# Rotary embedding in fp32: GpSimd and VectorE share the arithmetic in place of bf16 arithmetic between ScalarE casts

## The chip, the cores and the metric

One Trainium2 chip, one of its cores. The metric is the device time of one execution in microseconds (us), the median of several. All runs quoted here are of the fast state, at a granted clock of 1.0. The profile shows a span from the first to the last instruction. DVE is VectorE, ACT is ScalarE, POOL is GpSimd, SP is SyncE. SBUF and PSUM are the on-chip memories in which the kernels' tiles lie. The profile leaves numbers out of tile names: its t_ps and t_sb are the kernel's t1_ps and t2_sb.

## The reference

```python
x: (16, 512, 1024) fp32          # batch, seq, 16 heads of 64
cos, sin: (512, 32) fp32
x = x.reshape(16, 512, 16, 64)
x1, x2 = x[..., :32], x[..., 32:]
c, s = cos[None, :, None, :], sin[None, :, None, :]
out = concatenate([x1 * c - x2 * s, x1 * s + x2 * c], axis=-1)   # fp32
```

33.55 MB are read and 33.55 MB are written, whatever the arithmetic. Each element takes two multiplications and one addition or subtraction. A *row* below is one sequence position in each of the 128 partitions, an SBUF tile of 128x1024 fp32 (512 KB). There are 64 rows.

## The kernel before

A tile is one batch: four rows, 2 MB. The last two batches are split into two and four pieces. SyncE loads, ScalarE casts fp32 to bf16, VectorE does four bf16 operations, ScalarE casts back to fp32 and issues the store.

```python
# (cut: tile list, buffers, semaphores)
@block.sync
def _(sp):
    for t in range(NT):
        ...
        if t >= NX:                              # NX = 3 buffers of x
            sp.wait_ge(sem_ci, t - NX + 1)       # cast of the tile that held it
        sp.dma_start(x_sb[:, xb, 0:E], x_tile_ap(t)).then_inc(sem_in[xb], 16)
        ...                                      # t == 0: cos and sin after it
@block.scalar
def _(ae):
    ...                                          # tables to bf16
    for it in range(NT + LEAD):                  # LEAD = 2
        ...
            ae.wait_ge(sem_vf, u + 1)
            ...
            ae.activation(o_sb[:, ob, 0:Eu], ob_sb[:, obb, 0:Eu], ACT_COPY).then_inc(sem_co, 1)   # L129
            ae.wait_ge(sem_co, u + 1)
            ae.dma_start(out_tile_ap(u), o_sb[:, ob, 0:Eu]).then_inc(sem_out[ob], 16)
        ...
            ae.activation(xb_sb[:, cb, 0:E], x_sb[:, xb, 0:E], ACT_COPY).then_inc(sem_ci, 1)      # L143
@block.vector
def _(ve):
    for t in range(NT):
        ...
        ve.tensor_tensor(t1v, xbv, cos_b, mult)                              # bf16, L170
        ve.tensor_tensor(t2v, xbv, sin_b, mult).then_inc(sem_vp, 1)          # bf16, L171
        ...
        ve.tensor_tensor(obv[:, :, 0:HALF], t1[:, :, 0:HALF], t2[:, :, HALF:HD], subtract)
        ve.tensor_tensor(obv[:, :, HALF:HD], t2[:, :, 0:HALF], t1[:, :, HALF:HD], add).then_inc(sem_vf, 1)
```

## Time and profile before

| | before |
|---|---|
| measured time, median | 163.84 us |
| span of the profiled run | 162.1 us |
| busy: VectorE, ScalarE, GpSimd | 111.3, 118.6, 0.2 us |
| moved | 67.26 MB, 415 GB/s over the span |

First the profile page's busy times, then its slices. The span is cut into 40 equal slices of 4.05 us. Each digit is the busy share of a slice in tenths, 9 meaning 90% or more, and the last line is what the DMA engines moved in each.

```profile
DVE 111.3 (69%) x80; ACT 118.6 (73%) x45; POOL 0.2 (0%) x4
...
DVE  0006997989898989896939488492966994635450
ACT  3078389898989898967588775868859787445552
...
DMA  5999999999999999999999999999999999999985
GB/s 158 417 429 449 421 421 412 429 437 421 437 437 425 433 437 421 437 437 425 433 437 417 441 437 414 441 437 417 441 417 427 437 421 444 436 409 423 426 360 212
```

The DMA row is a solid line of nines from the second slice to the 38th, at 410 to 450 GB/s. No other row is. The engines that compute have gaps everywhere. This kernel is limited by its transfers.

The chain of waits agrees in its second half. It follows back what the last instruction depended on. First its shares of the span by engine, then a stretch of it; the columns are start, length and what it was.

```profile
DMA 54%; ACT 30%; issue 7%; DVE 5%; ACTq 1%; SPq 0%; DVEq 0%
...
66.12 24.16 DMA x_sb<-in_x_dram
90.28 0.02 issue
90.30 3.63 ACT xb_sb L143
93.93 0.02 issue
93.95 25.51 DMA x_sb<-in_x_dram
```

These two loads last 24 and 26 us, because three loads at a time and the stores share what the DMA engines moved, 431 GB/s from 60 to 100 us (loads land 9.7 us apart here, at 70.8, 80.6 and 90.3 us; the median of all 2 MB loads is 16.8 us). One cast (3.63 us) frees a buffer, and the next load starts at once. In the first half, up to 66 us, the chain runs through ScalarE instead, from cast to cast: it has 30% of the whole. Which of the two limits the kernel, the chain alone does not settle; the copy without arithmetic, e4 below, does.

Two groups of instructions on the page show what the change takes away (busy time in us, then the mean of one in ns):

```profile
L143 ACT ACTIVATE xb_sb<-x_sb 128x4096 bf16<-128x4096 f32 (+2 forms) x20 | 58.7, 2933 | 19.9 <-DMA x_sb<-in_x_dram 17.1
...
L129 ACT ACTIVATE o_sb<-ob_sb 128x4096 f32<-128x4096 bf16 (+2 forms) x20 | 58.6, 2929 | 12.7 <-DMA out_dram<-o_sb 7.5
```

The casts are 117 us of ScalarE work. What ended most of ScalarE's idle time is in both lines a DMA: ScalarE waits for transfers. But the load queue waits for casts too, in total (us), times, and longest wait:

```profile
SPq L100 <- ACT xb_sb L143: 132.3, 17, 10.3
```

Each load needs the buffer that a cast frees, so each side waits for the other. The DMA row shows that the DMA engines were kept busy all the same.

### The profile page before, as it was taken

How to read it: one execution, taken by the hardware profiler on the slowest of the kernel's cores; microseconds unless marked ns; L12 is line 12 of the kernel's file. 1: busy time of each engine (PE TensorE's matmuls, PEld its weight loads, DVE VectorE, ACT ScalarE, POOL GpSimd, SP SyncE). 2: the span in 40 equal slices, each digit the busy share in tenths (PEclk: the TensorE clock that was granted, in tenths of full speed). 3: DMA queues.
4: the chain of work that ended last, by engine and by line, in shares of the span. 5: the costliest groups of instructions: out<-in, count | busy, mean ns of one | idle time of the engine just before them, and what ended most of it. 6: DMA issues, size and time to landing. Idle time of an engine off the chain costs nothing.

```text
span 162.1 us, 266 instructions
## 1 busy us (share of the span) xinstructions
DVE 111.3 (69%) x80; ACT 118.6 (73%) x45; POOL 0.2 (0%) x4
## 2 busy tenths in 40 slices
DVE  0006997989898989896939488492966994635450
ACT  3078389898989898967588775868859787445552
POOL 0000000000000000000000000000000000000000
DMA  5999999999999999999999999999999999999985
GB/s 158 417 429 449 421 421 412 429 437 421 437 437 425 433 437 421 437 437 425 433 437 417 441 437 414 441 437 417 441 417 427 437 421 444 436 409 423 426 360 212
DMA packets 6050, 67.26 MB, mean 415 GB/s; under 512 B 672, under 2 KB 928, under 8 KB 1952
## 3 DMA queue, kind: packets, MB, share of 16 engines
q1 hardware_dynamic: 3168, 33.69, 49.5%
q10 hardware_dynamic: 2880, 33.56, 48.6%
q14 instruction: 2, 0.02, 0.0%
HBM read 33.69 MB, written 33.55 MB: 415 GB/s over the span
## 4 chain that ended last, share of the span: by engine, by line
DMA 54%; ACT 30%; issue 7%; DVE 5%; ACTq 1%; SPq 0%; DVEq 0%
DMA x_sb<-in_x_dram 49%; ACT xb_sb L143 15%; ACT o_sb L129 14%; DMA sin_sb<-in_sin_dram 5%; DVE tmp_sb L171 2%; DVE tmp_sb L170 1%; ACTq L133 1%; DVE ob_sb L176 1%; DVE ob_sb L179 1%; SPq L102 0%; SPq L100 0%; DVEq L55 0%; ACT coscat_sb L112 0%; ACT sincat_sb L115 0%; ACT coscat_sb L113 0%
## 5 line engine op out<-in xcount | busy, mean ns | idle before, releaser
L143 ACT ACTIVATE xb_sb<-x_sb 128x4096 bf16<-128x4096 f32 (+2 forms) x20 | 58.7, 2933 | 19.9 <-DMA x_sb<-in_x_dram 17.1
L170 DVE TENSOR_TENSOR tmp_sb<-xb_sb,coscat_sb 128x4096 bf16<-128x4096 bf16 (+2 forms) x20 | 37.3, 1865 | 45.8 <-ACT xb_sb L143 45.8
L129 ACT ACTIVATE o_sb<-ob_sb 128x4096 f32<-128x4096 bf16 (+2 forms) x20 | 58.6, 2929 | 12.7 <-DMA out_dram<-o_sb 7.5
L171 DVE TENSOR_TENSOR tmp_sb<-xb_sb,sincat_sb 128x4096 bf16<-128x4096 bf16 (+2 forms) x20 | 37.1, 1857 | 0.0
L176 DVE TENSOR_TENSOR ob_sb<-tmp_sb 128x2048 bf16<-128x2048 bf16 (+2 forms) x20 | 20.2, 1011 | 0.7
L179 DVE TENSOR_TENSOR ob_sb<-tmp_sb 128x2048 bf16<-128x2048 bf16 (+2 forms) x20 | 20.1, 1004 | 0.0
L112 ACT ACTIVATE coscat_sb<-cos_sb 128x128 bf16<-128x128 f32 x1 | 0.3, 309 | 7.0 <-DMA sin_sb<-in_sin_dram 7.0
L112 ACT ACT_TABLE_LOAD x1 | 1.3, 1283 | 0.7 <-PEq L197 0.7
L113 ACT ACTIVATE coscat_sb<-cos_sb 128x128 bf16<-128x128 f32 x1 | 0.3, 293 | 0.0
L115 ACT ACTIVATE sincat_sb<-sin_sb 128x128 bf16<-128x128 f32 x1 | 0.3, 293 | 0.0
L114 ACT ACTIVATE sincat_sb<-sin_sb 128x128 bf16<-128x128 f32 x1 | 0.3, 292 | 0.0
L197 POOL MEMSET const-bfloat16-1.0<- 128x1 bf16 x1 | 0.1, 101 | 0.0
L197 POOL MEMSET const-uint8-127<- 128x1 uint8 x1 | 0.1, 101 | 0.0
L197 POOL MEMSET const-float32-0.0<- 128x1 f32 x1 | 0.1, 98 | 0.2 <-issue 0.2
L197 POOL MEMSET const-float32-1.0<- 128x1 f32 x1 | 0.1, 98 | 0.0
## 6 DMA issues: line engine op xcount, KB each, us to landing
x_sb<-in_x_dram SPq DMA_DIRECT2D x14, 2048.0 KB, 16.8
out_dram<-o_sb ACTq DMA_DIRECT2D x14, 2048.0 KB, 19.7
x_sb<-in_x_dram SPq DMA_DIRECT2D x2, 1024.0 KB, 21.9
x_sb<-in_x_dram SPq DMA_DIRECT2D x4, 512.0 KB, 16.0
out_dram<-o_sb ACTq DMA_DIRECT2D x2, 1024.0 KB, 12.4
out_dram<-o_sb ACTq DMA_DIRECT2D x4, 512.0 KB, 3.6
cos_sb<-in_cos_dram SPq DMA_DIRECT2D x1, 64.0 KB, 7.3
sin_sb<-in_sin_dram SPq DMA_DIRECT2D x1, 64.0 KB, 7.3
```

The source lines that it names most:

```text
L112: last = ae.activation(coscat_sb[:, :, 0:HALF], cos_sb[:, :, :], ACT_COPY)
L113: last = ae.activation(coscat_sb[:, :, HALF:HD], cos_sb[:, :, :], ACT_COPY)
L114: last = ae.activation(sincat_sb[:, :, 0:HALF], sin_sb[:, :, :], ACT_COPY)
L115: last = ae.activation(sincat_sb[:, :, HALF:HD], sin_sb[:, :, :], ACT_COPY)
L129: ae.activation(o_sb[:, ob, 0:Eu], ob_sb[:, obb, 0:Eu], ACT_COPY).then_inc(sem_co, 1)
L133: ae.dma_start(out_tile_ap(u), o_sb[:, ob, 0:Eu]).then_inc(sem_out[ob], 16)
L143: ae.activation(xb_sb[:, cb, 0:E], x_sb[:, xb, 0:E], ACT_COPY).then_inc(sem_ci, 1)
L170: ve.tensor_tensor(t1v, xbv, cos_b, mult)
L171: ve.tensor_tensor(t2v, xbv, sin_b, mult).then_inc(sem_vp, 1)
L176: ve.tensor_tensor(obv[:, :, 0:HALF], t1[:, :, 0:HALF], t2[:, :, HALF:HD], subtract)
L179: ve.tensor_tensor(obv[:, :, HALF:HD], t2[:, :, 0:HALF], t1[:, :, HALF:HD], add).then_inc(sem_vf, 1)
L197: nc = _bacc.Bacc("TRN2", target_bir_lowering=False, num_devices=1)
```

## The change

The intent: drop the casts and stay in fp32. 64 rows go through a ring of 40 rows in SBUF, so loads can run far ahead, and the result is written over x. GpSimd forms x times sine (two instructions of 128x512 per row). VectorE forms x times cosine into PSUM and adds the two products. The cosine table lies in PSUM, so that no VectorE operation reads two operands from SBUF. ScalarE only prepares the sine table and issues stores. The first and last four rows move in smaller chunks (1, 1, 2 and 2, 1, 1 rows).

```diff
 # (cut: buffers, semaphores, the removed code shown above)
+    sizes = [[1, 1, 2]] + [[4]] * (G - 2) + [[2, 1, 1]]
+    RING = 40
+    NT1 = 3
+    NT2 = 4
+        c_ps = stack.enter_context(nc.psum_tensor([P, R, HALF], fp32))
+        t1_ps = stack.enter_context(nc.psum_tensor([P, NT1, 2 * H, HALF], fp32))
         @block.sync       # one load per chunk; waits only for the store that frees its rows
         @block.scalar
-            ... casts ...
+            ae.dma_start(stage[:, 0, :], cos...).then_inc(sem_cos, 16)
+            ae.dma_start(stage[:, 1, :], sin...).then_inc(sem_sin, 16)
+            ae.wait_ge(sem_sin, 16)
+            # (cut) s_sb[..., 0, :] = -sin, s_sb[..., 1, :] = sin, then_inc(sem_s, 1)
+            for c, (g, r, n, slot, at) in enumerate(chunks):
+                ae.wait_ge(sem_v, at + n)
+                ae.dma_start(ov[g, :, r:r + n, :], xs[:, slot:slot + n, :]).then_inc(sem_out[c], 16)
+        @block.gpsimd
+            for u in range(NU):                                   # NU = 64 rows
+                # (cut) wait for the load, the sine table, a free product buffer
+                for t in range(2):
+                    ins = pl.tensor_tensor(                        # L119, 128x512 fp32
+                        t2_sb[:, u % NT2, :, t, :],
+                        x_sb[:, k, :, 1 - t, :],
+                        s_sb[:, r, None, t, :].broadcast_to([P, H, HALF]), mult)
+                ins.then_inc(sem_p, 1)
         @block.vector
+            def mul(u):                                            # L145, 128x1024 fp32
+                if u == at: ve.wait_ge(sem_in[c], 16)
+                if u >= NT1: ve.wait_ge(sem_v, u - NT1 + 1)
+                ve.tensor_tensor(t1_ps[:, u % NT1, :, :], x_sb[:, k, ...], c_ps[:, r, ...], mult).then_inc(sem_m, 1)
+            def comb(u):                                           # L158, 128x1024 fp32
+                ve.wait_ge(sem_m, u + 1)
+                ve.wait_ge(sem_p, u + 1)
+                ve.tensor_tensor(x_sb[:, k, ...], t1_ps[:, u % NT1, :, :], t2_sb[:, u % NT2, ...], add).then_inc(sem_v, 1)
+            LEAD = 2
+            for u in range(NU + LEAD):
+                if u < NU: mul(u)
+                if u >= LEAD: comb(u - LEAD)
```

More of the change, by code (lines that the diff above doesn't have):

```diff
@@ L20, in bass_split_heads_rope_kernel @@
     P = 128
-    assert seq % P == 0
-    SPP = seq // P
-    tiles = [(b, 0, SPP) for b in range(batch)]
-    def _split(tile, parts):
-        b, j0, nj = tile
-        if nj % parts != 0:
-            return [tile]
-        q = nj // parts
-        return [(b, j0 + i * q, q) for i in range(parts)]
-    if len(tiles) >= 2:
-        t_last = tiles.pop()
-        t_prev = tiles.pop()
-        tiles += _split(t_prev, 2) + _split(t_last, 4)
-    NT = len(tiles)
-    ROWS = SPP * H
-    RE = ROWS * HD
@@ L42, in bass_split_heads_rope_kernel @@
-    NX = 3
-    NC = 3
-    NO = 3
-    NOB = 3
-    NTMP = 2
+    R = 4
+    SB = seq // R
+    BL = P // SB
+    G = batch // BL
+    assert SB * R == seq and BL * SB == P and G * BL == batch
     fp32 = mybir.dt.float32
-    bf16 = mybir.dt.bfloat16
     mult = mybir.AluOpType.mult
     add = mybir.AluOpType.add
-    subtract = mybir.AluOpType.subtract
-    ACT_COPY = mybir.ActivationFunctionType.Copy
-    with ExitStack() as stack:
-        cos_sb = stack.enter_context(nc.sbuf_tensor([P, SPP, HALF], fp32))
-        sin_sb = stack.enter_context(nc.sbuf_tensor([P, SPP, HALF], fp32))
-        coscat_sb = stack.enter_context(nc.sbuf_tensor([P, SPP, HD], bf16))
-        sincat_sb = stack.enter_context(nc.sbuf_tensor([P, SPP, HD], bf16))
-        x_sb = stack.enter_context(nc.sbuf_tensor([P, NX, RE], fp32))
-        xb_sb = stack.enter_context(nc.sbuf_tensor([P, NC, RE], bf16))
-        o_sb = stack.enter_context(nc.sbuf_tensor([P, NO, RE], fp32))
-        ob_sb = stack.enter_context(nc.sbuf_tensor([P, NOB, RE], bf16))
-        tmp1_sb = stack.enter_context(nc.sbuf_tensor([P, NTMP, ROWS, HD], bf16))
-        tmp2_sb = stack.enter_context(nc.sbuf_tensor([P, NTMP, ROWS, HD], bf16))
-        sem_tab = stack.enter_context(nc.semaphore("sem_tab"))
-        sem_tab2 = stack.enter_context(nc.semaphore("sem_tab2"))
-        sem_in = [stack.enter_context(nc.semaphore(f"sem_in{i}")) for i in range(NX)]
-        sem_out = [stack.enter_context(nc.semaphore(f"sem_out{i}")) for i in range(NO)]
-        sem_ci = stack.enter_context(nc.semaphore("sem_ci"))
-        sem_co = stack.enter_context(nc.semaphore("sem_co"))
-        sem_vp = stack.enter_context(nc.semaphore("sem_vp"))
-        sem_vf = stack.enter_context(nc.semaphore("sem_vf"))
-        block = stack.enter_context(nc.Block(no_gpsimd_drain=False))
-        cos_v = cos.rearrange("(p j) d -> p (j d)", p=P)
-        sin_v = sin.rearrange("(p j) d -> p (j d)", p=P)
-        def x_tile_ap(t):
-            b, j0, nj = tiles[t]
-            v = x[b, :, :].rearrange("(p j) d -> p j d", p=P)
-            return v[:, j0:j0 + nj, :].rearrange("p j d -> p (j d)")
-        def out_tile_ap(t):
-            b, j0, nj = tiles[t]
-            v = out[b, :, :, :].rearrange("(p j) h d -> p j (h d)", p=P)
-            return v[:, j0:j0 + nj, :].rearrange("p j e -> p (j e)")
-        def uses(nbuf, b):
-            return (NT - b + nbuf - 1) // nbuf
@@ new lines, in bass_split_heads_rope_kernel @@
+    COPY = mybir.ActivationFunctionType.Copy
+    sizes = [[1, 1, 2]] + [[4]] * (G - 2) + [[2, 1, 1]]
+    RING = 40
+    chunks = []
+    at = 0
+    for g, ss in enumerate(sizes):
+        r = 0
+        for n in ss:
+            slot = at % RING
+            assert slot + n <= RING
+            chunks.append((g, r, n, slot, at))
+            r += n
+            at += n
+        assert r == R
+    NC = len(chunks)
+    NU = at
+    unit_chunk = []
+    for c, (_, _, n, _, _) in enumerate(chunks):
+        unit_chunk += [c] * n
@@ new lines, in bass_split_heads_rope_kernel @@
+    NT1 = 3
+    NT2 = 4
+    with ExitStack() as stack:
+        x_sb = stack.enter_context(nc.sbuf_tensor([P, RING, H, 2, HALF], fp32))
+        t2_sb = stack.enter_context(nc.sbuf_tensor([P, NT2, H, 2, HALF], fp32))
+        stage = stack.enter_context(nc.sbuf_tensor([SB, 2, R * HALF], fp32))
+        s_sb = stack.enter_context(nc.sbuf_tensor([P, R, 2, HALF], fp32))
+        c_ps = stack.enter_context(nc.psum_tensor([P, R, HALF], fp32))
+        t1_ps = stack.enter_context(nc.psum_tensor([P, NT1, 2 * H, HALF], fp32))
+        sem_in = [stack.enter_context(nc.semaphore(f"in{c}")) for c in range(NC)]
+        sem_out = [stack.enter_context(nc.semaphore(f"out{c}")) for c in range(NC)]
+        sem_cos = stack.enter_context(nc.semaphore("cos"))
+        sem_sin = stack.enter_context(nc.semaphore("sin"))
+        sem_c = stack.enter_context(nc.semaphore("ctab"))
+        sem_s = stack.enter_context(nc.semaphore("stab"))
+        sem_p = stack.enter_context(nc.semaphore("pool"))
+        sem_m = stack.enter_context(nc.semaphore("mul"))
+        sem_v = stack.enter_context(nc.semaphore("comb"))
+        block = stack.enter_context(nc.Block(no_gpsimd_drain=False))
+        xv = x.rearrange("(g b) (s r) d -> g (b s) r d", b=BL, r=R)
+        ov = out.rearrange("(g b) (s r) h d -> g (b s) r (h d)", b=BL, r=R)
+        xs = x_sb[:].rearrange("p n h t d -> p n (h t d)")
@@ L92, in _ @@
         @block.sync
         def _(sp):
-            for t in range(NT):
-                xb = t % NX
-                _, _, nj = tiles[t]
-                E = nj * H * HD
-                if t >= NX:
-                    sp.wait_ge(sem_ci, t - NX + 1)
-                sp.dma_start(x_sb[:, xb, 0:E], x_tile_ap(t)).then_inc(sem_in[xb], 16)
-                if t == 0:
-                    sp.dma_start(
-                        cos_sb[:].rearrange("p j d -> p (j d)"), cos_v
-                    ).then_inc(sem_tab, 16)
-                    sp.dma_start(
-                        sin_sb[:].rearrange("p j d -> p (j d)"), sin_v
-                    ).then_inc(sem_tab, 16)
+            for c, (g, r, n, slot, at) in enumerate(chunks):
+                for e, (_, _, m, eslot, eat) in enumerate(chunks):
+                    if eat < at and eat + RING >= at and eslot < slot + n and slot < eslot + m:
+                        if eat + RING < at + n and eat + m + RING > at:
+                            sp.wait_ge(sem_out[e], 16)
+                sp.dma_start(xs[:, slot:slot + n, :], xv[g, :, r:r + n, :]).then_inc(sem_in[c], 16)
@@ L109, in _ @@
         @block.scalar
         def _(ae):
-            ae.wait_ge(sem_tab, 32)
-            last = ae.activation(coscat_sb[:, :, 0:HALF], cos_sb[:, :, :], ACT_COPY)
-            last = ae.activation(coscat_sb[:, :, HALF:HD], cos_sb[:, :, :], ACT_COPY)
-            last = ae.activation(sincat_sb[:, :, 0:HALF], sin_sb[:, :, :], ACT_COPY)
-            last = ae.activation(sincat_sb[:, :, HALF:HD], sin_sb[:, :, :], ACT_COPY)
-            last.then_inc(sem_tab2, 1)
-            LEAD = 2
-            for it in range(NT + LEAD):
-                u = it - LEAD
-                if u >= 0:
-                    ob = u % NO
-                    obb = u % NOB
-                    _, _, nju = tiles[u]
-                    Eu = nju * H * HD
-                    ae.wait_ge(sem_vf, u + 1)
-                    if u >= NO:
-                        ae.wait_ge(sem_out[ob], 16 * (u // NO))
-                    ae.activation(
-                        o_sb[:, ob, 0:Eu], ob_sb[:, obb, 0:Eu], ACT_COPY
-                    ).then_inc(sem_co, 1)
-                    ae.wait_ge(sem_co, u + 1)
-                    ae.dma_start(out_tile_ap(u), o_sb[:, ob, 0:Eu]).then_inc(sem_out[ob], 16)
-                t = it
-                if t < NT:
-                    xb = t % NX
-                    cb = t % NC
-                    _, _, nj = tiles[t]
-                    E = nj * H * HD
-                    ae.wait_ge(sem_in[xb], 16 * (t // NX + 1))
-                    if t >= NC:
-                        ae.wait_ge(sem_vp, t - NC + 1)
-                    ae.activation(
-                        xb_sb[:, cb, 0:E], x_sb[:, xb, 0:E], ACT_COPY
-                    ).then_inc(sem_ci, 1)
@@ L146, in _ @@
-            for b in range(NO):
-                ae.wait_ge(sem_out[b], 16 * uses(NO, b))
+            ae.dma_start(stage[:, 0, :], cos.rearrange("(s r) d -> s (r d)", r=R)).then_inc(sem_cos, 16)
+            ae.dma_start(stage[:, 1, :], sin.rearrange("(s r) d -> s (r d)", r=R)).then_inc(sem_sin, 16)
+            ae.wait_ge(sem_sin, 16)
+            sv = stage[:, 1, :].rearrange("s (r d) -> s r d", d=HALF)
+            for lo, hi in ((0, R),):
+                for q in range(BL):
+                    ps = slice(q * SB, (q + 1) * SB)
+                    ae.activation(s_sb[ps, lo:hi, 0, :], sv[:, lo:hi, :], COPY, scale=-1.0)
+                    ae.activation(s_sb[ps, lo:hi, 1, :], sv[:, lo:hi, :], COPY).then_inc(sem_s, 1)
@@ new lines, in _ @@
+            for c, (g, r, n, slot, at) in enumerate(chunks):
+                ae.wait_ge(sem_v, at + n)
+                ae.dma_start(ov[g, :, r:r + n, :], xs[:, slot:slot + n, :]).then_inc(sem_out[c], 16)
+            for c in range(NC):
+                ae.wait_ge(sem_out[c], 16)
+        @block.gpsimd
+        def _(pl):
+            for u in range(NU):
+                c = unit_chunk[u]
+                g, r0, n, slot, at = chunks[c]
+                r = r0 + u - at
+                k = slot + u - at
+                if u == at:
+                    pl.wait_ge(sem_in[c], 16)
+                if u == 0:
+                    pl.wait_ge(sem_s, BL)
+                if u >= NT2:
+                    pl.wait_ge(sem_v, u - NT2 + 1)
+                for t in range(2):
+                    ins = pl.tensor_tensor(
+                        t2_sb[:, u % NT2, :, t, :],
+                        x_sb[:, k, :, 1 - t, :],
+                        s_sb[:, r, None, t, :].broadcast_to([P, H, HALF]),
+                        mult,
+                    )
+                ins.then_inc(sem_p, 1)
@@ L149, in _ @@
         @block.vector
         def _(ve):
-            for t in range(NT):
-                bt, j0, nj = tiles[t]
-                R = nj * H
-                E = R * HD
-                cb = t % NC
-                tb = t % NTMP
-                obb = t % NOB
-                if t == 0:
-                    ve.wait_ge(sem_tab2, 1)
-                ve.wait_ge(sem_ci, t + 1)
-                if t >= NTMP:
-                    ve.wait_ge(sem_vf, t - NTMP + 1)
-                xbv = xb_sb[:, cb, 0:E].rearrange("p (j h d) -> p j h d", j=nj, h=H)
-                t1 = tmp1_sb[:, tb, 0:R, :]
-                t2 = tmp2_sb[:, tb, 0:R, :]
-                t1v = t1.rearrange("p (j h) d -> p j h d", j=nj)
-                t2v = t2.rearrange("p (j h) d -> p j h d", j=nj)
-                cos_b = coscat_sb[:, j0:j0 + nj, None, :].broadcast_to([P, nj, H, HD])
-                sin_b = sincat_sb[:, j0:j0 + nj, None, :].broadcast_to([P, nj, H, HD])
-                ve.tensor_tensor(t1v, xbv, cos_b, mult)
-                ve.tensor_tensor(t2v, xbv, sin_b, mult).then_inc(sem_vp, 1)
-                ve.wait_ge(sem_vp, t + 1)
-                if t >= NOB:
-                    ve.wait_ge(sem_co, t - NOB + 1)
-                obv = ob_sb[:, obb, 0:E].rearrange("p (r d) -> p r d", d=HD)
-                ve.tensor_tensor(
-                    obv[:, :, 0:HALF], t1[:, :, 0:HALF], t2[:, :, HALF:HD], subtract
-                )
-                ve.tensor_tensor(
-                    obv[:, :, HALF:HD], t2[:, :, 0:HALF], t1[:, :, HALF:HD], add
-                ).then_inc(sem_vf, 1)
@@ new lines, in _ @@
+            ve.wait_ge(sem_cos, 16)
+            cv = stage[:, 0, :].rearrange("s (r d) -> s r d", d=HALF)
+            for q in range(BL):
+                ins = ve.tensor_copy(c_ps[q * SB:(q + 1) * SB, :, :], cv)
+            ins.then_inc(sem_c, 1)
+            ve.wait_ge(sem_c, 1)
+            def mul(u):
+                c = unit_chunk[u]
+                g, r0, n, slot, at = chunks[c]
+                r = r0 + u - at
+                k = slot + u - at
+                if u == at:
+                    ve.wait_ge(sem_in[c], 16)
+                if u >= NT1:
+                    ve.wait_ge(sem_v, u - NT1 + 1)
+                ve.tensor_tensor(
+                    t1_ps[:, u % NT1, :, :],
+                    x_sb[:, k, :, :, :].rearrange("p h t d -> p (h t) d"),
+                    c_ps[:, r, None, :].broadcast_to([P, 2 * H, HALF]),
+                    mult,
+                ).then_inc(sem_m, 1)
@@ new lines, in comb @@
+            def comb(u):
+                c = unit_chunk[u]
+                g, r0, n, slot, at = chunks[c]
+                k = slot + u - at
+                ve.wait_ge(sem_m, u + 1)
+                ve.wait_ge(sem_p, u + 1)
+                ve.tensor_tensor(
+                    x_sb[:, k, :, :, :].rearrange("p h t d -> p (h t) d"),
+                    t1_ps[:, u % NT1, :, :],
+                    t2_sb[:, u % NT2, :, :, :].rearrange("p h t d -> p (h t) d"),
+                    add,
+                ).then_inc(sem_v, 1)
@@ L185 @@
+            LEAD = 2
+            for u in range(NU + LEAD):
+                if u < NU:
+                    mul(u)
+                if u >= LEAD:
+                    comb(u - LEAD)
 _INS = ['x', 'cos', 'sin', 'num_heads']
```

## The prediction

> **What bounds the kernel now.** The DMA engines. In the page's forty slices their busy share is 9 or more in slices 2 to 38 and they move 409 to 449 GB/s; 67.26 MB at about 430 GB/s take 156 us of the 162.1 us span. VectorE (111.3 us) and ScalarE (118.6 us) idle a third of it. The chain of waits says the same: 49% of it is "DMA x_sb<-in_x_dram", and from 66 us on it is almost only loads of 24 to 25 us each, alternating with one cast that frees the buffer. Outside the transfers lie about 2 us before the first bytes and the tail: the last store is issued at 158.9 us and ends at 162.1 us (3.2 us for 512 KB). The measured time is 1.7 us longer than the span.
>
> **What the change does.** It moves the same 67 MB, so the transfer floor stays at about 156 us plus start and tail, roughly 160 us. It removes ScalarE's 40 casts (117 us, none of it the limit except at the start: first compute on VectorE at 13.5 us, first store at 24.1 us). It makes the first load 512 KB and lets loads run 40 rows ahead. It adds fp32 arithmetic, in 64 units of 128x1024:
>
> - VectorE: two fp32 operations per unit, each with a PSUM operand. The present bf16 operations cost 692, 1221 and 2292 ns for 1024, 2048 and 4096 elements: 0.52 ns per element plus 157 ns. [...] Back to back, the trace hides about 80 ns of that (2.29 us long, 2.21 us apart); with a wait on the instruction just before, 40 ns come on top. In the new order each multiply waits for the add just before it (three t1 buffers, lead of two)[...].
> - GpSimd: two 128x512 fp32 multiplies per unit. Before has none to measure. [...]
> - [...] Here every VectorE operation has one in PSUM, so I expect no mutual slowing.
>
> **Critical path.** The transfer limit (about 154 to 156 us) is joined by a VectorE limit of 155 us and a GpSimd limit near 150 us. The early start buys the slack back: tables and first row land near 4 us, VectorE starts at 4 to 5 us and ends near 160 us, the last 512 KB store takes 3.2 us, the difference to the span 1.7 us: about 164.5 us. Gain from the shorter start and loss from the slower arithmetic cancel. I predict 164 us, 159.5 to 172; faster by over 2% 0.17, within 2% 0.53, slower 0.30.
>
> **What would show it.** VectorE busy above 90% with 1.2 us operations; GpSimd 85 to 98%; DMA share slightly under 9 in the middle, about 410 GB/s; loads finishing well before the end; the chain of waits mostly VectorE and GpSimd rather than loads; first VectorE arithmetic before 6 us; first store before 12 us.
>
> **What would make it wrong.** GpSimd above 1.25 us per instruction (each 0.1 us costs 13 us): slower, with VectorE's adds waiting for GpSimd. PSUM operands adding more than 0.1 us per VectorE operation. GpSimd and VectorE slowing each other after all. In the other direction, if both finish a unit in under 2.35 us, transfers bound again and the early start shows as about 160 us.

Terms are cut from the text above: how I sized an fp32 operation on VectorE and a multiplication on GpSimd rested on no trace of this case. The sums were 2.42 us per row and 155 us in all for VectorE, and 2.3 to 2.5 us per row and 147 to 160 us in all for GpSimd. With VectorE last, 4 to 5 us of start, 155, 3.2 for the last store and 1.7 from the span to the measured time make the "about 164.5 us". That an operand in PSUM keeps the two engines from slowing each other was not shown either when this was written; e7 and e6 below measure it.

## The result and the profile after

| | before | after |
|---|---|---|
| measured time, median | 163.84 us | 169.33 us |
| span of the profiled run | 162.1 us | 167.3 us |
| busy: VectorE, ScalarE, GpSimd | 111.3, 118.6, 0.2 us | 151.7, 1.8, 155.5 us |
| moved | 67.26 MB, 415 GB/s | 67.27 MB, 402 GB/s |

The change is slower: ratio 1.031, 95% interval 1.028 to 1.035. A ratio here is the one for the fast runs; it is not quite the ratio of the medians quoted (1.034 for the change).

The page of the change, the same lines as before, and GpSimd's (slices of 4.18 us):

```profile
DVE 151.7 (91%) x129; ACT 1.8 (1%) x3; POOL 155.5 (93%) x132
...
DVE  0689999999998999999999999999999999999942
...
POOL 0299999999999999999999999999999999999990
DMA  4999999999999999999999999999999999980895
GB/s 131 439 441 418 407 444 425 415 413 435 439 435 427 429 435 433 423 423 439 439 431 423 435 439 415 435 431 439 435 423 429 423 423 430 403 376 2 376 413 214
```

Now three rows are full of nines. DMA is as busy as before up to the 35th slice, and then has a hole: 2 GB/s in the 37th slice. The last load had landed at 145.7 us. From then on only stores are left, and they come at the pace of the arithmetic. So the transfers are not what ends last, though most of the page looks as if they were. The chain of waits decides:

```profile
POOL 83%; issue 9%; DMA 3%; POOLq 1%; DVE 1%; ACT 0%; ACTq 0%; DVEq 0%
POOL t_sb L119 83%; DMA stage<-in_sin_dram 3%; POOLq L57 1%; DVE x_sb L158 1%; ACTq L90 0%; ACT s_sb L97 0%; ACT s_sb L98 0%; DVEq L157 0%; POOLq L115 0%
```

Where before it was loads, it is now GpSimd for 83% of the span. The groups of the page:

```profile
L119 POOL TENSOR_TENSOR t_sb<-x_sb,s_sb 128x512 f32<-128x512 f32 x128 | 155.3, 1254 | 7.0 <-ACT s_sb L98 7.0
L145 DVE TENSOR_TENSOR t_ps<-x_sb,c_ps 128x1024 f32<-128x1024 f32 x64 | 78.6, 1229 | 4.5 <-DMA x_sb<-in_x_dram 1.3
L158 DVE TENSOR_TENSOR x_sb<-t_ps,t_sb 128x1024 f32<-128x1024 f32 x64 | 78.0, 1219 | 2.7 <-POOL t_sb L119 2.3
```

GpSimd idles once, 7.0 us at the start, until the sine table is there, and never again. Its durations overlap, so they are not its pace. The view of the tile that it writes gives the first and the last start of the 128 instructions:

```profile
L119 POOL TENSOR_TENSOR t_sb<-x_sb,s_sb x128: 1242/1249/1286, 7.5 to 161.6; 128x512 f32<-128x512 f32 x128
```

(161.6 - 7.5) / 127 = 1.213 us from start to start, 2.43 us per row. So GpSimd is timed here by the spacing of starts and not by the reported duration. One of the experiments below, e7, shows why: at nearly the same spacing (1.212 us) the mean duration reads 1306 ns instead of 1254.

VectorE stands close behind. The timeline in the middle (start, length, what):

```profile
99.86 1.23 DVE L158 TENSOR_TENSOR x_sb<-t_ps,t_sb 128x1024 f32<-128x1024 f32 x1
101.19 1.23 DVE L145 TENSOR_TENSOR t_ps<-x_sb,c_ps 128x1024 f32<-128x1024 f32 x1
102.33 1.22 DVE L158 TENSOR_TENSOR x_sb<-t_ps,t_sb 128x1024 f32<-128x1024 f32 x1
103.58 1.23 DVE L145 TENSOR_TENSOR t_ps<-x_sb,c_ps 128x1024 f32<-128x1024 f32 x1
```

From a multiply to the add is 1.14 us: the add waits for nothing recent and overlaps the multiply's end. From the add to the next multiply is 1.25 us (1.33 at a chunk's first row). That multiply waits for the add to have finished, because the add frees the third t1 buffer. So VectorE alone needs 2.39 us per row, and 2.41 on average with the chunk starts: 1% less than GpSimd.

The start and the end of the timeline give the rest of the sum (in brackets, how long the engine was idle before, and what ended that):

```profile
5.34 0.30 DVE L132 COPY c_ps<-stage 128x128 f32<-128x128 f32 x1 [5.34 <-DMA stage<-in_cos_dram]
...
6.83 0.31 ACT L97 ACTIVATE s_sb<-stage 128x128 f32<-128x128 f32 x1 [3.89 <-DMA stage<-in_sin_dram]
7.04 0.29 ACT L98 ACTIVATE s_sb<-stage 128x128 f32<-128x128 f32 x1
7.49 14.61 POOL L119 TENSOR_TENSOR t_sb<-x_sb,s_sb 128x512 f32<-128x512 f32 x12 [7.04 <-ACT s_sb L98]
```

```profile
160.48 1.22 DVE L158 TENSOR_TENSOR x_sb<-t_ps,t_sb 128x1024 f32<-128x1024 f32 x1 [1.13 <-POOL t_sb L119]
162.90 1.23 DVE L158 TENSOR_TENSOR x_sb<-t_ps,t_sb 128x1024 f32<-128x1024 f32 x1 [1.20 <-POOL t_sb L119]
```

7.5 us until GpSimd starts, 155.3 us of GpSimd, 1.3 us for the last add, and 3.1 us from the issue of the last store at 164.2 us to the end: 167.2 of the 167.3 us.

### The profile page after: what moved, and what is told of

Read it like the earlier page. It is cut to its first block, busy times and chain, and to the rows that moved or that the text cites. A ratio compares the mean times of both kernels' runs of the same rounds, so it can differ in the third digit from the quotient of the medians.

```text
span 167.3 us, 443 instructions
## 1 busy us (share of the span) xinstructions
DVE 151.7 (91%) x129; ACT 1.8 (1%) x3; POOL 155.5 (93%) x132
## 2 busy tenths in 40 slices
DMA packets 6052, 67.27 MB, mean 402 GB/s; under 512 B 673, under 2 KB 929, under 8 KB 1953
## 4 chain that ended last, share of the span: by engine, by line
POOL 83%; issue 9%; DMA 3%; POOLq 1%; DVE 1%; ACT 0%; ACTq 0%; DVEq 0%
POOL t_sb L119 83%; DMA stage<-in_sin_dram 3%; POOLq L57 1%; DVE x_sb L158 1%; ACTq L90 0%; ACT s_sb L97 0%; ACT s_sb L98 0%; DVEq L157 0%; POOLq L115 0%
## 5 line engine op out<-in xcount | busy, mean ns | idle before, releaser
L119 POOL TENSOR_TENSOR t_sb<-x_sb,s_sb 128x512 f32<-128x512 f32 x128 | 155.3, 1254 | 7.0 <-ACT s_sb L98 7.0
L145 DVE TENSOR_TENSOR t_ps<-x_sb,c_ps 128x1024 f32<-128x1024 f32 x64 | 78.6, 1229 | 4.5 <-DMA x_sb<-in_x_dram 1.3
L158 DVE TENSOR_TENSOR x_sb<-t_ps,t_sb 128x1024 f32<-128x1024 f32 x64 | 78.0, 1219 | 2.7 <-POOL t_sb L119 2.3
L97 ACT ACTIVATE s_sb<-stage 128x128 f32<-128x128 f32 x1 | 0.3, 311 | 3.9 <-DMA stage<-in_sin_dram 3.9
L98 ACT ACTIVATE s_sb<-stage 128x128 f32<-128x128 f32 x1 | 0.3, 294 | 0.0
```

Source lines behind the costliest of these rows:

```text
L97: ae.activation(s_sb[ps, lo:hi, 0, :], sv[:, lo:hi, :], COPY, scale=-1.0)
L98: ae.activation(s_sb[ps, lo:hi, 1, :], sv[:, lo:hi, :], COPY).then_inc(sem_s, 1)
L119: ins = pl.tensor_tensor(t2_sb[:, u % NT2, :, t, :], x_sb[:, k, :, 1 - t, :], s_sb[:, r, None, t, :].broadcast_to([P, H, HALF]), mult,)
L145: ve.tensor_tensor(t1_ps[:, u % NT1, :, :], x_sb[:, k, :, :, :].rearrange("p h t d -> p (h t) d"), c_ps[:, r, None, :].broadcast_to([P, 2 ...
L158: ve.tensor_tensor(x_sb[:, k, :, :, :].rearrange("p h t d -> p (h t) d"), t1_ps[:, u % NT1, :, :], t2_sb[:, u % NT2, :, :, :].rearrange("p ...
```

## The experiments

Twelve kernels ran, in four sets; each set ran on one chip, beside runs of the kernel before. The sets ran on different chips, and the change itself was not run again in them. The kernel before had medians of 163.71 to 163.85 us in them, so a difference of one or two tenths of a us between runs of different sets says nothing. Each edit is to the changed kernel unless it says otherwise. My theory G was that GpSimd's own rate and its late start set the time. The rivals were V, that VectorE's order, or a mutual slowing of the two engines, sets the pace of both, and D, that the transfers do.

| run | edit | median us | ratio to before |
|---|---|---|---|
| e1_pool_half | half of GpSimd's work (wrong result) | 167.43 | 1.022 |
| e2_sin_first | sine table requested first | 167.69 | 1.024 |
| e3_pool_pair | two rows per GpSimd instruction | 169.33 | 1.034 |
| e4_copy_only | no arithmetic (wrong result) | 163.06 | 0.996 |
| e5_lead1 | add one row behind the multiply | 169.29 | 1.032 |
| e6_cos_sbuf | cosine table in SBUF | 230.29 | 1.404 |
| e7_no_mul | VectorE multiplies the first three rows only (wrong result) | 169.22 | 1.032 |
| e8_combo | e2, e3 and e5 together | 163.86 | 0.999 |
| e9_no_pair | e2 and e5 | 168.05 | 1.026 |
| e10_no_lead1 | e2 and e3 | 167.81 | 1.025 |
| e11_no_sin_first | e3 and e5 | 163.98 | 1.002 |
| e12_big_first | e8 with a first load of four rows | 165.09 | 1.008 |

### Is GpSimd's rate its own? e7_no_mul and e1_pool_half

```diff
 # e7_no_mul, in mul(u) and comb(u)
                 if u >= NT1:
-                    ve.wait_ge(sem_v, u - NT1 + 1)
+                    return
-                ve.wait_ge(sem_m, u + 1)
+                ve.wait_ge(sem_m, min(u + 1, NT1))
```

> VectorE multiplies only the first three rows and adds in all 64 (wrong result on purpose), so VectorE is half free. Theory G, GpSimd's rate is its own: its instructions stay 1.210 to 1.215 us apart, end within 0.3 us of before, 168.9 to 169.4 us. Rival V, VectorE with one SBUF input slows GpSimd: they come closer together than 1.19 us, and the time falls below 167.

Measured 169.22 us, against 169.33 for the change. The groups of its page:

```profile
L119 POOL TENSOR_TENSOR t_sb<-x_sb,s_sb 128x512 f32<-128x512 f32 x128 | 155.2, 1306 | 7.1 <-ACT s_sb L98 7.1
L158 DVE TENSOR_TENSOR x_sb<-t_ps,t_sb 128x1024 f32<-128x1024 f32 x64 | 78.4, 1224 | 75.4 <-POOL t_sb L119 75.4
```

GpSimd's train is 155.2 us long with VectorE half idle, and 155.3 us with VectorE full. The starts are 1.212 us apart, all of them between 1.210 and 1.224, whether an add runs beside them or not. VectorE now waits 75.4 us for GpSimd. So VectorE's operations with one SBUF input did not slow GpSimd here (1.213 us apart in the change, 1.212 with half of them gone), and GpSimd alone is enough to give the measured time. V's second half, mutual slowing, falls.

```diff
 # e1_pool_half, GpSimd
+            pl.memset(t2_sb[:, :, :, 1, :], 0.0)
-                for t in range(2):
+                for t in range(1):
```

> GpSimd does one of its two multiplications per row; the other half of its product is zero (wrong result on purpose). Theory G (GpSimd's own rate is the limit: 128 instructions, 1.213 us apart, never waiting): GpSimd falls to about 78 us and stops mattering, but VectorE stands right behind at 2.39 to 2.42 us per row (multiply waits for the add just before it); it starts at 5.7 us, ends near 160.5, so about 165.5 to 166.5 us instead of 169.3. Theory V (VectorE and GpSimd slow each other): VectorE's 1.22 us operations get shorter by 5% or more and the time falls below 163. Theory D (transfers are the limit, their share is 9 tenths until 145 us): time stays at 169.

Measured 167.43 us, 1.9 us less, and 1 us above what I expected. With GpSimd's work halved only this little is gained, because VectorE takes over: its multiply and add still take 1229 and 1218 ns, and its rows come 2.41 us apart. I had missed the tail. At the end the last three adds follow each other 1.13 us apart (3.48 us for the three), so their stores are handed to the DMA engines in a burst:

```profile
157.33 3.48 DVE L159 TENSOR_TENSOR x_sb<-t_ps,t_sb 128x1024 f32<-128x1024 f32 x3
```

From the issue of the last store (160.84 us) to the end (165.56 us) it is 4.7 us, against 3.1 us in the change.

### Is the late start on the path? e2_sin_first

```diff
-            ae.dma_start(stage[:, 0, :], cos...).then_inc(sem_cos, 16)
             ae.dma_start(stage[:, 1, :], sin...).then_inc(sem_sin, 16)
+            ae.dma_start(stage[:, 0, :], cos...).then_inc(sem_cos, 16)
```

> The sine table is requested before the cosine table. Theory G: GpSimd's 128 multiplications are one unbroken train that starts when the sine table is there (7.49 us); sine lands about 0.5 to 1 us earlier, so the end comes as much earlier: 168.3 to 168.9 us. Theories V and D: VectorE's start comes later or nothing changes at the limit: 169.3 or more.

Measured 167.69 us: 1.64 us less, below the range that I expected. GpSimd's first start moved from 7.49 to 5.99 us, 1.5 us earlier, more than I had guessed, and the end of the last add moved with it, from 164.1 to 162.6 us.

```profile
5.99 8.53 POOL L119 TENSOR_TENSOR t_sb<-x_sb,s_sb 128x512 f32<-128x512 f32 x7 [5.55 <-ACT s_sb L98]
```

VectorE starts 1.5 us later (7.15 us), which costs nothing. This agrees with G. V and D both predicted no gain.

### GpSimd's cost per instruction: e3_pool_pair

```diff
-    NT2 = 4
+    NT2 = 8
 # GpSimd steps over pairs of rows, w = 2 (w = 1 in chunks of one row); cut: the waits, counted in pairs
-                        t2_sb[:, u % NT2, :, t, :],
-                        x_sb[:, k, :, 1 - t, :],
-                        s_sb[:, r, None, t, :].broadcast_to([P, H, HALF]), mult)
+                        t2_sb[:, j:j + w, :, t, :],
+                        x_sb[:, k:k + w, :, 1 - t, :],
+                        s_sb[:, r:r + w, None, t, :].broadcast_to([P, w, H, HALF]), mult)
```

> GpSimd multiplies two rows per instruction (128x1024 instead of 128x512), half as many instructions, ring of products 8 instead of 4. Theory G with a fixed cost per instruction near 0.1 us: about 2.32 us per instruction, 148 us in all; then VectorE (2.40 us per row) sets the time: 165.5 to 167 us. If there is no fixed cost (2.42 us per instruction): 169.3. Theory D: 169.3.

Measured 169.33 us: not a microsecond gained, which is what D expected. It would have been easy to conclude that GpSimd is not the limit. The trace says otherwise. GpSimd's 128x1024 instructions start 2.28 us apart, against 1.210 us for 128x512 at its closest. An estimate from these two spacings: an instruction costs about 0.14 us, and an element 2.09 ns: (2.281 - 1.210) / 512. GpSimd saved 8.6 us (146.9 us busy instead of 155.5), and no longer ends last. The end of its timeline:

```profile
147.03 7.17 POOL L128 TENSOR_TENSOR t_sb<-x_sb,s_sb 128x1024 f32<-128x1024 f32 x5
...
159.22 3.48 DVE L168 TENSOR_TENSOR x_sb<-t_ps,t_sb 128x1024 f32<-128x1024 f32 x3
```

GpSimd is done at 154.2 us and VectorE at 162.7. VectorE had waited 1.8 us for the first pair, then ran at its own 2.41 us per row. And, as in e1, the bunched last adds give a tail of 4.7 us. So the arithmetic ended 1.4 us earlier than in the change (162.7 instead of 164.1), because VectorE stands right behind GpSimd, and the tail took 1.6 us more. That the two cancel, and the total stays the same, is a coincidence.

### VectorE's order alone: e5_lead1

```diff
-            LEAD = 2
+            LEAD = 1
```

With the add one row behind the multiply, a multiply of row u needs the add of row u - 3, which is no longer the instruction just before it.

> VectorE adds one row behind its multiply instead of two, so with three t1 buffers no operation waits for the one just before it. Theory G (GpSimd's 128 instructions, 1.213 us apart from 7.49 us on, set the end): time stays at 169.0 to 169.5, VectorE's rows follow GpSimd at 2.43 us with waits on GpSimd showing. Rival V (VectorE's own order, 2.39 to 2.41 us per row, sets the pace of both): rows at 2.28 us and about 162 to 164 us.

Measured 169.29 us, between 168.89 and 169.57: no gain, as G says. The first half of V falls too: VectorE's order is not the only limit. The rows are 2.43 us apart like GpSimd's. The waits show less clearly than I had expected: the list of waits puts only 3.3 us on GpSimd, since most of them are about 0.15 us long each (a row takes 2.43 us here, and 2.26 to 2.31 us where VectorE waits for nothing, in e8).

### What the transfers allow: e4_copy_only

```diff
 # ScalarE: a chunk is stored as soon as it has landed; GpSimd and VectorE do nothing
-                ae.wait_ge(sem_v, at + n)
+                ae.wait_ge(sem_in[c], 16)
```

> No arithmetic: each chunk is stored as soon as it has landed, same ring, same sizes (wrong result on purpose). This is the floor of the transfers. Theory G or V: 159 to 162 us, clearly below 169. Theory D: 166 to 169.

Measured 163.06 us. This is 6.3 us below the change, so D falls. But it is 1 us above the range in which I expected the floor. Its slices:

```profile
DMA  4999999999999999999999999999999999999996
GB/s 126 427 412 420 437 425 425 431 427 435 419 439 439 415 443 435 423 435 423 443 431 415 447 439 415 439 431 431 435 419 439 439 415 431 428 425 432 430 417 251
```

The kernel before took 163.71 us. It was 0.4% above what a plain copy through the ring of the change needs. With transfers of this form (these sizes, one queue for loads and one for stores) there was almost nothing to win. Whether another form of the transfers is faster was not tested, apart from the first load in e12.

### The three together, and each left out: e8_combo to e11_no_sin_first

> Sine first, two rows per GpSimd instruction with eight product buffers, add one row behind the multiply: all three limits lifted together. GpSimd 2.28 us per row from 6.0 us, VectorE 2.28 to 2.30 us per row from 7.2 us, both done near 155 if data were there; then the transfers bind, whose floor without arithmetic measured 163.06: 163.0 to 164.5 us. If any of the three was not a limit of its own, it stays above 165.5.

Measured 163.86 us with a correct result: 5.5 us less than the change, although e3 and e5 alone gained nothing and e2 1.6 us. Against the kernel before it is a tie: ratio 0.999, interval 0.9975 to 1.0006.

```profile
GB/s 123 432 437 421 424 404 431 425 425 437 433 421 431 437 425 429 437 429 429 433 433 429 433 433 425 439 429 425 433 437 421 435 431 417 435 427 443 421 407 200
...
L128 POOL TENSOR_TENSOR t_sb<-x_sb,s_sb 128x1024 f32<-128x1024 f32 (+1 forms) x68 | 146.8, 2198 | 5.8 <-ACT s_sb L104 5.7
L168 DVE TENSOR_TENSOR x_sb<-t_ps,t_sb 128x1024 f32<-128x1024 f32 x64 | 78.1, 1221 | 1.4 <-POOL t_sb L128 1.4
L155 DVE TENSOR_TENSOR t_ps<-x_sb,c_ps 128x1024 f32<-128x1024 f32 x64 | 77.9, 1219 | 0.0
```

The hole in the transfers is gone. The last store is issued at 155.1 us, and the DMA engines need nearly until the end at 161.9 us to work off what is queued. VectorE's operations start 1.13 us apart, in both directions, and its rows 2.28 us.

> The combination without its larger GpSimd instructions: sine first, add one row behind, GpSimd one row at a time. GpSimd's 128 instructions at 1.213 us from 6.0 us end near 161.3 us: 167.4 to 168.0 us. If VectorE's order had been the real limit of the change: about 164.

Measured 168.05 us, slightly above the range. GpSimd's 128 small instructions set the end again.

> The combination without the new order on VectorE: sine first, two rows per GpSimd instruction, add two rows behind. VectorE's 2.39 to 2.41 us per row from 7.15 us end near 161 us: 165.8 to 166.6 us, GpSimd idle at the end. If GpSimd alone had been the limit: about 164.

Measured 167.81 us: VectorE ends last, at 161.2 us as expected, but the time is 1.2 us above the range. I had again counted 3.2 us for the tail; it is 4.7 us, as in e1 and e3.

> The combination with the cosine table first as in the change. GpSimd from 7.5 us at 2.28 us per row ends near 154 us, VectorE soon after, both before the transfers: 163.7 to 164.5 us, equal to the combination within 0.4 us. If the early start is still worth its 1.6 us: 165.3 or more.

Measured 163.98 us. Once both engines are faster than the transfers, the early sine table is worth 0.1 us by the medians (0.4 us by the ratios, as the sets differ) and no longer 1.6. So the two arithmetic limits have to be lifted together, and then the start hardly matters: the last store is issued 1.5 us later than in e8 (156.5 us), but the transfers still queued end at nearly the same time (span 162.1 and 161.9 us).

### The table in PSUM: e6_cos_sbuf

```diff
-        c_ps = stack.enter_context(nc.psum_tensor([P, R, HALF], fp32))
+        c_ps = stack.enter_context(nc.sbuf_tensor([P, R, HALF], fp32))
```

> The cosine table lies in SBUF instead of PSUM, nothing else changes, so VectorE's multiply has two SBUF inputs. If [...]GpSimd's two multiplications (2.43 us) and VectorE's multiply (1.14 to 1.23 us) of a row cannot overlap, 3.6 to 3.7 us per row, 235 to 250 us in all. If there is no contention in this pairing: 169.3.

Measured 230.29 us, 61 us more than the change and a little less than expected.

```profile
L119 POOL TENSOR_TENSOR t_sb<-x_sb,s_sb 128x512 f32<-128x512 f32 x128 | 216.1, 1727 | 7.4 <-ACT s_sb L98 7.4
L145 DVE TENSOR_TENSOR t_ps<-x_sb,c_ps 128x1024 f32<-128x1024 f32 x64 | 140.5, 2196 | 4.5 <-DMA x_sb<-in_x_dram 1.2
L158 DVE TENSOR_TENSOR x_sb<-t_ps,t_sb 128x1024 f32<-128x1024 f32 x64 | 77.5, 1211 | 2.5 <-POOL t_sb L119 2.5
```

Only VectorE's multiply changed its operands, and it takes 2196 ns instead of 1229; the add is unchanged. On GpSimd the starts alternate, 1.21 us and 2.19 us apart: one of a row's two instructions is held up by about 0.98 us, and a row takes 3.41 us. One after the other, without any overlap, the spacings of the row's two GpSimd instructions and VectorE's multiply in the change would add up to 3.56 us (2 x 1.21 + 1.14), an estimate. So in this run the multiply with two SBUF inputs and GpSimd's instructions slowed each other nearly as if they had run in turn (3.41 us); with one SBUF input (e7) no slowing showed. By what mechanism, the traces do not show. The choice of PSUM for the table was right, and worth 61 us of this design.

### A larger first load: e12_big_first

```diff
-    sizes = [[1, 1, 2]] + [[4]] * (G - 2) + [[2, 1, 1]]
+    sizes = [[4]] * (G - 1) + [[2, 1, 1]]                # on top of e8_combo
```

> The combination with its first load in one piece of four rows (2 MB, as in the kernel before) instead of 1, 1 and 2 rows. In the first of forty slices the kernel before moves 158 GB/s, the combination 123: worth about 0.35 us of transfer. If transfers alone bind, the later start of the arithmetic (about 3 us) is hidden by the ring and this gives 163.3 to 163.9 us, a tie with the kernel before within 0.4%. If arithmetic still has no slack, it gets slower: 165 or more.

Measured 165.09 us: slower than e8. The tie that I hoped for did not come; it is the other branch of what I wrote. The start of its timeline shows why.

```profile
8.84 0.31 ACT L103 ACTIVATE s_sb<-stage 128x128 f32<-128x128 f32 x1 [5.91 <-DMA stage<-in_sin_dram]
...
13.95 0.29 DVE L142 COPY c_ps<-stage 128x128 f32<-128x128 f32 x1 [13.95 <-DMA stage<-in_cos_dram]
14.28 2.36 DVE L155 TENSOR_TENSOR t_ps<-x_sb,c_ps 128x1024 f32<-128x1024 f32 x2
```

The cosine table, 64 KB on ScalarE's own queue, lands at 13.9 us instead of 7.1. I had counted only on x landing later. VectorE starts 6.8 us later than in e8, and that is more than the slack: the last add ends at 159.2 us, and the DMA rate falls to 297 GB/s in the 37th slice: the arithmetic ends last again. Why the 2 MB load delays the tables is not shown; that they land later beside it, is: from issue to landing the two tables of 64 KB took 4.6 and 5.6 us beside the first loads of 512 KB in the change, and 8.1 and 12.8 us here. The landing times in the traces show a pattern: in the change and in all twelve runs the first table requested landed 0.2 us after the first load of x, and the second 0.2 to 0.6 us after the second. Those loads landed at 5.1 and 6.6 us in the change, and at 8.6 and 13.7 us here. No version beat the kernel before.

## Why the prediction was right or wrong

The measured 169.33 us lie in the stated range of 159.5 to 172 us. My middle, 164.0, was 5.3 us low, and I gave "slower" only 0.30. The range held because it was wide: the path that I wrote down, with VectorE last, is not the one that ran. The text names the right danger, a slow GpSimd with VectorE's adds waiting for it, but from 1.25 us per instruction on; 1.213 us was enough.

- *The transfers limit the kernel before.* Right: a copy without arithmetic takes 163.06 us and the kernel before 163.71. The casts, 117 us of ScalarE, do stand in the first half of its chain of waits, but taking them away gained nothing: even the copy is only 0.65 us faster.
- *The transfer floor: "roughly 160 us" plus 1.7.* Too low by about 1.4 us: 163.06 measured. This small term decides the sign: with these transfers even arithmetic that costs no time would have won 0.4%, so the 0.17 that I gave to "faster by over 2%" had no ground.
- *VectorE: 1.2 us per operation, a full wait at each multiply, 2.42 us per row.* Right: 1.229 and 1.219 us, 2.39 within a chunk, 2.41 on average. That e8 removes this wait and gets 2.28 us confirms the mechanism.
- *GpSimd: 2.3 to 2.5 us per row, 147 to 160 us.* The range holds: 2.43 us, 155.3 us. But in "Critical path" I carried it on as "a GpSimd limit near 150 us", 5 us short, so that VectorE alone seemed to end last. That was the mis-sized term: 150 us are 1.17 us for each of the 128 instructions, and 1.213 us was measured, of which the estimate from e3 puts 0.14 us down to the instruction and not to its elements. The text itself gave the sensitivity: "each 0.1 us costs 13 us".
- *Start: "tables and first row land near 4 us, VectorE starts at 4 to 5 us".* The other mis-sized term. The cosine table was used at 5.34 us, and the sine table landed at 6.8 us, behind it; GpSimd, the limiting engine, starts at 7.49 us. e2 shows that this start is paid in full: 1.5 us earlier, 1.64 us less.
- *The sum.* Predicted: end of VectorE "near 160 us". Measured: 7.5 + 155.3 + 1.3 = 164.1 us. The last term is new: the last add cannot begin before GpSimd's last product, and I had not counted it. The store (3.2 predicted, 3.1 measured) and the difference to the span (1.7 and 1.8) were right.
- *No mutual slowing.* Right, by e7: GpSimd's starts are 1.212 us apart with VectorE half idle and 1.213 in the change. The reason given, one operand in PSUM, agrees with e6: with the table in SBUF a row takes 3.41 us instead of 2.43.
- *Signs.* VectorE above 90% (91%), GpSimd 85 to 98% (93%), loads done well before the end (145.7 us), chain mostly GpSimd, first VectorE arithmetic before 6 us (5.67), first store before 12 us (11.5): as written. "About 410 GB/s in the middle" was wrong; it is about 430 (424 to 432 in each 20 us from 20 to 140 us), because the ring lets loads run ahead, and most of the missing transfers are in one hole near 152 us.

## What to carry to other kernels

When a kernel's DMA row is nines from end to end, first run the same transfers without arithmetic: here that showed 0.4% of room before any redesign. When two or three limits lie within 1% of each other, lifting one can show nothing (e3 and e5: 0.0 us each) and lifting them together much (e11, these two alone: 5.35 us), so read in the trace which engine ends last after each edit before dropping a theory. Here the engine that ran without a gap paid for its late start in full (e2) and for about 0.14 us in each of its instructions (the estimate from e3); give such an engine its inputs first, and fewer, larger instructions.
